# Three modulation parts of a hybrid decoder: their sums moved from VectorE to ScalarE and GpSimd

## The chip, the cores and the metric

One core of a Trainium2 chip runs the whole program. The metric is the device time of one execution in microseconds (us). PE is TensorE (matmuls), DVE is VectorE, ACT is ScalarE, POOL is GpSimd, SP is the queue that issues the DMAs here. Times given as positions are microseconds from the start of the profiled span.

## The reference

The model has two layers. Each has an attention (stick-breaking in the first layer, softmax with forgetting in the second) and a gated MLP with a short causal convolution, for 512 positions of width 1024 and 16 heads of 64. The change concerns the conditioning: a vector c of 1024 values is turned by a matrix of 1024 x 6144 for each layer into six vectors of 1024, which scale, shift and gate the two halves of the layer.

```python
c_act = jax.nn.silu(c)
for i in range(DEPTH):                                    # DEPTH = 2
    mod = jnp.einsum('bd,dm->bm', c_act, w_mod[i]) + b_mod[i]
    sh_a, sc_a, gt_a, sh_f, sc_f, gt_f = jnp.split(mod, N_MOD, axis=-1)
    h = modulate(rmsnorm(x, g_mix_pre[i]), sh_a, sc_a)
    ...                                                   # attention of h, 16 heads
    x = x + gt_a[:, None, :] * rmsnorm(o, g_mix_post[i])
    h = modulate(rmsnorm(x, g_ffn_pre[i]), sh_f, sc_f)
    ...                                                   # gated MLP of h
    x = x + gt_f[:, None, :] * rmsnorm(y, g_ffn_post[i])
```

The first attention computes, for each head and query t, weights that are a sigmoid of the score times the product of (1 - sigmoid) over the keys between; the sum of logarithms in the reference is a running product in the kernel.

## The kernel before

All matrices are float32. A float32 operand is split into a high part in the fp32r format and the rest (`split`, L191: ACT casts the high part, DVE or POOL subtracts), and each product is three matmuls (`mm3`, L264: L266, L267, L268).

**Modulation.** One part, such as GT_A of layer 0, is a sum over 1024 rows of w_mod, 1024 wide. `mod_part` (L130) loads it as eight tiles `wm` of 128 x 1024 (L139). On each partition the tile is multiplied by that partition's value of silu(c), a column of `csil`, and added into `acc` (L143; the first tile of a part with L141, unless the part is a row part whose `acc` starts from a POOL memset and the bias, L135 and L136). `acc` is then split into `ah` (ACT, L146) and `al` (DVE, L148), and two matmuls with a matrix of ones per half (L160, L161) add up the 128 partitions into `pm`. GT parts are kept as rows (L163, times the gain `gp`), the others as columns (the diagonal reads of L128, then L169 and L171). The generator yields after each tile, so that the caller decides how far a part goes at a time.

The `wm` tiles, `ah`, `al` and `gp` share one pool of three buffers (`t4`), `acc` has one buffer.

**Where the parts run.** Two parts (SH_A, SC_A of layer 0) are made by the opening `begin`, in another way. The three parts GT_A, SC_F and SH_F of layer 0 go through a `Background` that `attention` (L519) steps: three steps after each head from the third head on (L559). The remaining six go through a second `Background` inside layer 0's MLP (L831, L870), and the last, of layer 1, likewise.

**The first attention** (some 65 to 290 us). For each head and each of four query blocks TensorE makes the scores `ps` (L380), ACT two sigmoids (L389, L390), DVE a running product `om` (the scan, L391), and POOL (the two larger blocks) or DVE (the two smaller) the product `bt` (L392). In the next head's turn TensorE transposes these (`pa`, L414), ACT and DVE split the result (`ah`, `al`, L192, L193), and TensorE makes the head's output `po` (L429, L430). ACT and DVE bring it into place (`of`, L434, L435; per pair of heads split into `oh`, `ol`). Between these, a `Filler` gives TensorE the projections of later heads (`pqk`, `pv`), whose weights are loaded by SP (`wf`, L198), cast by ACT (`wh`) and subtracted by POOL (`wl`), through three buffers each; queries and keys are then split by ACT, DVE and POOL (`qa`, `qb`, L358, L359; `kh`, `kl`, L368 to L371).

**Order.** PE and SP run in the order of the program (`manual_schedule`). ACT, DVE and POOL are put in order by a planner with costs of its own; what `bg.step` issues within the attention is given a lower priority there (an offset of -100). Every engine executes its own queue strictly in order.

Of the kernel before, what the change touches and what calls it, by code (L numbers as in the profile page):

```python
# [11 lines left out]
AF = mybir.ActivationFunctionType  # L12
ALU = mybir.AluOpType
# [20 lines left out]
SH_A, SC_A, GT_A, SH_F, SC_F, GT_F = range(6)  # L34
# [3 lines left out]
def trunk(ctx, tc, x, c, w_mod, b_mod, g_mix_pre, g_mix_post, w_qkv, w_o, w_fg, b_fg,  # L38
          g_ffn_pre, g_ffn_post, w_gate, w_up, w_conv, b_conv, w_down, out):
    nc = tc.nc  # L40
# [6 lines left out]
    def nm(s):  # L47
        serial[0] += 1
        return f"{s}_{serial[0]}"

    def bank(s="b"):
        return pp.tile([P, 512], F32, tag="bank", name=nm(s), bufs=8)
# [7 lines left out]
    def t4(s, dt=F32):  # L60
        return sb.tile([P, D], dt, tag="t4", name=nm(s), bufs=3)
# [26 lines left out]
    csil = cst.tile([P, ND], F32, name="csil")  # L88
# [6 lines left out]
    def b_col(l, comp):  # L95
        return colA[:, 48 * l + 8 * comp : 48 * l + 8 * comp + 8]

    def g_col(l, comp):
        o = (96 if comp == SC_A else 112) + 8 * l
        return colA[:, o : o + 8]  # L100
# [25 lines left out]
    def diagonal(dst, src):  # L126

        nc.vector.tensor_tensor_reduce(junk(P), src, idn, 1.0, 0.0, op0=ALU.mult, op1=ALU.add, accum_out=dst)  # L128

    def mod_part(l, comp):  # L130
        row = comp in (GT_A, GT_F)
        acc = sb.tile([P, D], F32, tag="acc", name=nm("acc"), bufs=1)
        lo_c = comp * D
        if row:
            nc.gpsimd.memset(acc, 0.0)  # L135
            nc.sync.dma_start(acc[0:1, :], b_mod[l : l + 1, lo_c : lo_c + D])  # L136
        for d in range(ND):
            w = t4("wm")
            nc.sync.dma_start(w, w_mod[l, d * P : (d + 1) * P, lo_c : lo_c + D])  # L139
            if d == 0 and not row:  # L140
                nc.vector.tensor_scalar(acc, w, csil[:, 0:1], None, op0=ALU.mult)  # L141
            else:
                nc.vector.scalar_tensor_tensor(acc, w, csil[:, d : d + 1], acc, op0=ALU.mult, op1=ALU.add)  # L143
            yield
        ah = t4("ah", F32R)
        nc.scalar.copy(ah, acc)  # L146
        al = t4("al", F32R)
        nc.vector.tensor_tensor(al, acc, ah.bitcast(F32), op=ALU.subtract)  # L148
        if row:
            res = sb.tile([P, D], F32, tag="gt", name=nm("gt"), bufs=2)  # L150
            gp = t4("gp")
            g = (g_mix_post if comp == GT_A else g_ffn_post)[l]
            nc.sync.dma_start(gp, g.rearrange("(o n) -> o n", o=1).to_broadcast([P, D]))
        else:
            res = cst.tile([P, ND], F32, name=nm("mc"))
        yield
        for h in range(2):
            cs = slice(512 * h, 512 * h + 512)
            ps = bank("pm")
            nc.tensor.matmul(ps, ones, ah[:, cs], start=True, stop=False)  # L160
            nc.tensor.matmul(ps, ones, al[:, cs], start=False, stop=True)  # L161
            if row:
                nc.vector.tensor_tensor(res[:, cs], ps, gp[:, cs], op=ALU.mult)  # L163
            else:
                for j in range(4):
                    diagonal(res[:, 4 * h + j : 4 * h + j + 1], ps[:, j * P : (j + 1) * P])
            yield
        if not row:
            nc.vector.tensor_tensor(res, res, b_col(l, comp), op=ALU.add)  # L169
            if comp in (SC_A, SC_F):  # L170
                nc.vector.scalar_tensor_tensor(res, res, 1.0, g_col(l, comp), op0=ALU.add, op1=ALU.mult)  # L171
        made[l, comp] = res

    class Background:
        def __init__(self, parts):
            self.gens = [mod_part(*p) for p in parts]

        def step(self, n=1):
            while n and self.gens:
# [575 lines left out]

    cums_of = {}
    for l in range(DEPTH):
        bg = Background([(l, GT_A), (l, SC_F), (l, SH_F)] if l == 0 else [])
        scale = -0.125 if l % 2 else 0.125
        vt, qk = {}, {}  # L760
        if l == 0:
# [69 lines left out]
        bg = Background([(l, GT_F)] + ([(l + 1, c_) for c_ in (SC_A, SH_A, SC_F, SH_F, GT_A)] if l + 1 < DEPTH else []))  # L831
# [102 lines left out]
```

## Time and profile before

| | |
|---|---|
| median of 3 runs | 1308.4 us (1306.46 to 1308.93) |
| profiled execution | 1311.87 us, its span 1310.1 us |
| mean granted TensorE clock | 0.99 |
| busy of the span | PE 95%, DVE 63%, ACT 47%, POOL 22% |
| HBM | 165.92 MB read, 2.16 MB written |

How to read it: a busy share over the whole span is a mean over stages with different limits. A TensorE that is 95% busy has about 61 us in which it is not; the question for a change is which stage these lie in and what ended each wait. Rows give the line of the kernel, the engine, the operation, the output, the inputs and the shapes; an arrow to the left names what ended a wait.

### The profile page before, as it was taken

What the parts mean: (1) busy time and instruction counts of PE and PEld (TensorE: products, weight loads), DVE (VectorE), ACT (ScalarE), POOL (GpSimd) and SP (SyncE); (2) the same over time, 40 slices, a digit from 0 to 9 for tenths busy, and PEclk for the clock granted to TensorE, in tenths of its full rate; (3) what the DMA queues carried; (4) which work ended last, traced back from release to release, by engine and by line L of the source; (5) the groups of instructions that cost most, each with busy time, mean ns of one, the idle gap of its engine ahead of it and who ended that gap; (6) DMA issues with size and microseconds to landing.
All of it is one profiled execution on the core that took longest, in us unless ns stands there. A gap on an engine that the chain in (4) does not pass through costs nothing.

```text
span 1310.1 us, 17095 instructions
## 1 busy us (share of the span) xinstructions
PE 1249.2 (95%) x6244; PEld 1048.3 (80%) x6244; DVE 821.9 (63%) x1447; ACT 615.8 (47%) x1182; POOL 292.2 (22%) x326
## 2 busy tenths in 40 slices
PE   5888978999999999999999999999999999999997
PEld 3766857789888788888888789887898888888886
DVE  7778889756869887532344777786775444443233
ACT  5566745756434343321356556666753333332121
POOL 3676444641000000000023744554100000000000
PEclk8999989999999999999999999999999999999999
DMA  8653433222657776332411533332254333333321
GB/s 264 207 174 101 153 121 130 78 69 64 225 192 258 227 239 215 106 97 97 143 36 47 165 113 107 103 117 80 78 192 130 97 97 97 97 97 97 97 97 65
DMA packets 174856, 169.19 MB, mean 129 GB/s; under 512 B 6936, under 2 KB 151728, under 8 KB 174772
## 3 DMA queue, kind: packets, MB, share of 16 engines
q1 hardware_dynamic: 174596, 168.04, 40.8%
q8 instruction: 49, 0.80, 0.3%
q14 instruction: 35, 0.29, 0.1%
q10 hardware_dynamic: 176, 0.07, 0.0%
HBM read 165.92 MB, written 2.16 MB: 128 GB/s over the span
## 4 chain that ended last, share of the span: by engine, by line
PE 71%; DVE 13%; DMA 6%; ACT 5%; issue 3%; POOL 1%; SPq 0%; POOLq 0%; DVEq 0%; ACTq 0%
PE pgu L267 11%; PE pgu L268 11%; PE pgu L266 11%; PE pd L266 6%; PE pd L268 6%; PE pd L267 6%; DMA wm<-in_w_mod_dram 3%; PE pqk L266 2%; PE pqk L267 2%; PE pqk L268 2%; PE ps L380 2%; DVE acc L143 2%; PE pa L414 2%; PE po L266 1%; PE po L268 1%
## 5 line engine op out<-in xcount | busy, mean ns | idle before, releaser
L192 ACT CAST wh<-wf 128x1024 fp32r<-128x1024 f32 (+2 forms) x178 | 185.3, 1041 | 316.6 <-PE pgu L267 140.7
L193 DVE TENSOR_TENSOR wl<-wf,wh 128x1024 fp32r<-128x1024 f32 x122 | 149.2, 1223 | 217.7 <-ACT wh L192 215.6
L267 PE MATMUL pgu<-htl,wh 128*128 128x512 f32 (+1 forms) x736 | 276.4, 375 | 0.2
L266 PE MATMUL pgu<-hth,wh 128*128 128x512 f32 (+1 forms) x736 | 276.3, 375 | 0.0
L268 PE MATMUL pgu<-hth,wl 128*128 128x512 f32 (+1 forms) x736 | 276.2, 375 | 0.0
L193 POOL TENSOR_TENSOR wl<-wf,wh 128x1024 fp32r<-128x1024 f32 (+3 forms) x56 | 133.5, 2388 | 221.7 <-ACT wh L192 214.0
L267 PEld LDWEIGHTS pgu<-htl,wh 128*128 128x128 f32 x736 | 138.6, 188 | 25.5 <-DVE htl L328 0.6
L266 PEld LDWEIGHTS pgu<-hth,wh 128*128 128x128 f32 x736 | 138.6, 188 | 25.0
L268 PEld LDWEIGHTS pgu<-hth,wl 128*128 128x128 f32 x736 | 138.5, 188 | 25.0
L279 POOL TENSOR_TENSOR r<-v,mhalf 128x1 f32<-128x1 f32 x32 | 17.8, 555 | 450.0 <-DVE v L275 450.0
L143 DVE SCALAR_TENSOR_TENSOR acc<-wm,csil,acc 128x1024 f32<-128x1024 f32 x74 | 101.7, 1374 | 18.2 <-DMA wm<-in_w_mod_dram 17.5
L267 PE MATMUL pd<-wl,yh 128*128 128x512 f32 x288 | 112.0, 389 | 0.0
L266 PE MATMUL pd<-wh,yh 128*128 128x512 f32 x288 | 112.0, 389 | 0.0
L268 PE MATMUL pd<-wh,yl 128*128 128x512 f32 x288 | 112.0, 389 | 0.0
L266 PE MATMUL pqk<-hth,wh 128*128 128x512 f32 (+1 forms) x240 | 100.7, 420 | 0.3 <-DVE al L193 0.3
L268 PE MATMUL pqk<-hth,wl 128*128 128x512 f32 (+1 forms) x240 | 93.6, 390 | 0.1
L267 PE MATMUL pqk<-htl,wh 128*128 128x512 f32 (+1 forms) x240 | 93.5, 389 | 0.0
L846 ACT ACTIVATE cv<-cv 128x512 f32<-128x512 f32 x44 | 27.8, 633 | 102.6 <-DVE cv L845 98.2
L266 PE MATMUL pv<-wh,hth 128*128 128x256 f32 (+1 forms) x224 | 70.7, 316 | 1.1 <-ACT wh L192 0.6
L267 PE MATMUL pv<-wl,hth 128*128 128x256 f32 (+1 forms) x224 | 67.7, 302 | 1.2 <-POOL wl L193 1.2
L268 PE MATMUL pv<-wh,htl 128*128 128x256 f32 (+1 forms) x224 | 67.7, 302 | 0.1
L268 PEld LDWEIGHTS pd<-wh,yl 128*128 128x128 f32 x288 | 54.1, 188 | 11.3
(194 smaller groups left out, 2474.7 us busy)
## 6 DMA issues: line engine op xcount, KB each, us to landing
wm<-in_w_mod_dram SPq DMA_DIRECT2D x80, 512.0 KB, 4.9
wf<-in_w_ffn_gate_dram SPq DMA_DIRECT2D x44, 512.0 KB, 4.2
wf<-in_w_ffn_up_dram SPq DMA_DIRECT2D x44, 512.0 KB, 3.8
wf<-in_w_ffn_down_dram SPq DMA_DIRECT2D x44, 512.0 KB, 3.5
wf<-in_w_qkv_dram SPq DMA_DIRECT2D x41, 512.0 KB, 3.8
wm<-in_w_mod_dram SPq DMA_DIRECT2D x32, 256.0 KB, 4.6
wf<-in_w_o_dram SPq DMA_DIRECT2D x16, 512.0 KB, 3.5
cum<-cumd SPq DMA_DIRECT2D x16, 512.0 KB, 4.2
```

The costliest lines, as they stand in the source:

```text
L143: nc.vector.scalar_tensor_tensor(acc, w, csil[:, d : d + 1], acc, op0=ALU.mult, op1=ALU.add)
L192: nc.scalar.copy(hi, src)
L193: (engine or nc.vector).tensor_tensor(lo, src, hi.bitcast(F32), op=ALU.subtract)
L266: nc.tensor.matmul(ps, ah, bh, start=first, stop=False)
L267: nc.tensor.matmul(ps, ah, bl, start=False, stop=False)
L268: nc.tensor.matmul(ps, al, bh, start=False, stop=last)
L279: nc.gpsimd.tensor_tensor(r, v, mhalf, op=ALU.pow)
L380: nc.tensor.matmul(ps[:, :n], q[hd][:, qs], k[hd][i][:, :n], start=i == 0, stop=i == 1)
L414: nc.tensor.transpose(ps[:, (qb - kb) * P : (qb - kb + 1) * P], probs[qb][:, kb * P : (kb + 1) * P], idn)
L846: nc.scalar.activation(a, a, AF.Silu)
```

## The change

For the three parts beside the first attention, and for these alone, DVE's multiply-and-add of a tile is replaced by two instructions. ACT scales the tile by the column of `csil`: in place, or, for the first tile of a column part, directly into `acc`. POOL then adds the scaled tile to `acc`. The split of `acc`, the matmuls, the loads and their places in the program are as they were; the parts made in the MLP keep the DVE sums.

```diff
-    def mod_part(l, comp):
+    def mod_part(l, comp, beside):
...
             nc.sync.dma_start(w, w_mod[l, d * P : (d + 1) * P, lo_c : lo_c + D])
-            if d == 0 and not row:
+            if beside:
+                dst = acc if d == 0 and not row else w
+                nc.scalar.activation(dst, w, AF.Copy, scale=csil[:, d : d + 1])
+                if dst is w:
+                    nc.gpsimd.tensor_tensor(acc, acc, w, op=ALU.add)
+            elif d == 0 and not row:
                 nc.vector.tensor_scalar(acc, w, csil[:, 0:1], None, op0=ALU.mult)
             else:
                 nc.vector.scalar_tensor_tensor(acc, w, csil[:, d : d + 1], acc, op0=ALU.mult, op1=ALU.add)
...
     class Background:
-        def __init__(self, parts):
-            self.gens = [mod_part(*p) for p in parts]
+        def __init__(self, parts, beside=False):
+            self.gens = [mod_part(*p, beside) for p in parts]
...
-        bg = Background([(l, GT_A), (l, SC_F), (l, SH_F)] if l == 0 else [])
+        bg = Background([(l, GT_A), (l, SC_F), (l, SH_F)] if l == 0 else [], True)
```

## Prediction

> **What bounds the kernel now.** I read the page first: its busy shares and its chain that ended last.
>
> ```profile
> PE 1249.2 (95%) x6244; PEld 1048.3 (80%) x6244; DVE 821.9 (63%) x1447; ACT 615.8 (47%) x1182; POOL 292.2 (22%) x326
> PE 71%; DVE 13%; DMA 6%; ACT 5%; issue 3%; POOL 1%; SPq 0%; POOLq 0%; DVEq 0%; ACTq 0%
> ```
>
> TensorE bounds the whole, and DVE is second on the chain. So I looked for the stretch in which TensorE is idle, and asked for the busy times of two windows: 80 to 240 us, which holds every sum of the three modulation parts that run beside the first attention, and 240 to 300 us, the attention's end, which has none of them. The columns are the window, its length, then busy us (and instructions) by engine and the clock granted to TensorE.
>
> ```profile
> 80.00:240.00 160.00, 138.09 (x768) 115.78 (x767) 138.44 (x218) 96.09 (x213) 86.47 (x116) 0.96 0.41 135
> 240.00:300.00 60.00, 57.06 (x290) 47.25 (x288) 40.27 (x83) 37.34 (x83) 27.02 (x36) 1.00 0.28 84
> ```
>
> With the sums, TensorE idles 160 - 138.09 = 21.9 us and DVE is at 138.44/160 = 87%; without them TensorE idles 2.94 of 60 us (4.9%) and DVE is at 67%. Much of the idle time lies in a few large pieces. TensorE's timeline gives the four of over 2 us; the bracket is the idle time ahead of the instruction and what ended it.
>
> ```profile
> 168.44 0.47 PE L380 MATMUL ps<-kh,qb 128*128 128x128 f32 x1 [5.18 <-DVE om L391]
> 191.77 0.30 PE L414 MATMUL pa<-zid,bt 128*128 128x128 f32 x1 [2.66 <-DVE bt L392]
> 204.69 0.39 PE L430 MATMUL po<-al,v 128*128 128x256 f32 x1 [2.21 <-DVE al L193]
> 226.07 0.33 PE L380 MATMUL ps<-kh,qb 128*128 128x128 f32 x1 [2.42 <-DVE om L391]
> ```
>
> All four, 12.5 us together, end on a DVE instruction of the attention. What stood ahead of them on DVE, with the POOL instruction that ran beside the first:
>
> ```profile
> 161.54 1.64 DVE L143 SCALAR_TENSOR_TENSOR acc<-wm,csil,acc 128x1024 f32<-128x1024 f32 x1 [1.94 <-DMA wm<-in_w_mod_dram]
> 162.39 3.00 POOL L193 TENSOR_TENSOR wl<-wf,wh 128x1024 fp32r<-128x1024 f32 x1 [0.25 <-ACT wh L192]
> 163.11 2.82 DVE L193 TENSOR_TENSOR ol<-of,oh 128x512 fp32r<-128x512 f32 x1
> 165.86 1.27 DVE L143 SCALAR_TENSOR_TENSOR acc<-wm,csil,acc 128x1024 f32<-128x1024 f32 x1
> 167.16 1.22 DVE L391 TENSOR_TENSOR_SCAN om<-ps,zid 128x512 f32<-128x512 f32 x1
> 188.47 2.96 DVE L143 SCALAR_TENSOR_TENSOR acc<-wm,csil,acc 128x1024 f32<-128x1024 f32 x1 [0.57 <-DMA wm<-in_w_mod_dram]
> 201.28 2.42 DVE L143 SCALAR_TENSOR_TENSOR acc<-wm,csil,acc 128x1024 f32<-128x1024 f32 x1
> 221.13 1.28 DVE L143 SCALAR_TENSOR_TENSOR acc<-wm,csil,acc 128x1024 f32<-128x1024 f32 x1
> ```
>
> Each time a sum of L143 is directly or shortly ahead. The 5.18 us case shows the mechanism whole: DVE waits 1.94 us for a weight tile, sums, then its next instruction is held until POOL's ends at 165.39, sums again, and only at 167.16 gets to the scan that TensorE needs. After such an idle piece the clock is low for some microseconds:
>
> ```profile
> 168.00:172.00 4.00, 3.56 (x10) 2.75 (x11) 3.91 (x7) 1.23 (x5) 3.01 (x6) 0.50 0.21 73
> 190.00:194.00 4.00, 2.23 (x9) 1.94 (x10) 3.87 (x11) 1.01 (x2) 1.89 (x4) 0.85 0.38 99
> 194.00:198.00 4.00, 4.00 (x19) 3.32 (x18) 3.73 (x7) 2.05 (x5) 0.39 (x1) 0.73 0.22 61
> 226.00:230.00 4.00, 3.93 (x20) 3.71 (x21) 4.00 (x11) 1.81 (x8) 2.06 (x5) 0.61 0.01 4
> ```
>
> Busy time by the share not granted: 3.56 x 0.50 + 2.23 x 0.15 + 4.00 x 0.27 + 3.93 x 0.39 = 1.78 + 0.33 + 1.08 + 1.53 = 4.7 us.
>
> **The change part by part.** The rows that carry the prices, grouped by shape in the window 80 to 240 us (count, then busy us and mean ns of one, then idle time before; the line with three slashed figures is one of the whole trace, shortest, median and longest ns):
>
> ```profile
> L143 DVE SCALAR_TENSOR_TENSOR acc<-wm,csil,acc 128x1024 f32<-128x1024 f32 x22 | 35.1, 1594 | 5.4 <-DMA wm<-in_w_mod_dram 5.3
> L141 DVE TENSOR_SCALAR acc<-wm,csil 128x1024 f32<-128x1024 f32 x2 | 1.7, 872 | 0.0
> L193 DVE TENSOR_TENSOR ol<-of,oh 128x512 fp32r<-128x512 f32 x5 | 5.6, 1114 | 0.7 <-ACT oh L192 0.7
> L193 DVE TENSOR_TENSOR ol<-of,oh x16: 684/692/2823, 114.8 to 912.2; 128x512 fp32r<-128x512 f32 x16
> L148 DVE TENSOR_TENSOR al<-acc,ah 128x1024 fp32r<-128x1024 f32 x3 | 4.6, 1518 | 1.4 <-ACT ah L146 1.4
> L146 ACT CAST ah<-acc 128x1024 fp32r<-128x1024 f32 x3 | 3.1, 1041 | 0.2 <-DVE acc L143 0.2
> L193 POOL TENSOR_TENSOR wl<-wf,wh 128x1024 fp32r<-128x1024 f32 x15 | 39.4, 2628 | 23.6 <-ACT wh L192 23.3
> L392 POOL TENSOR_TENSOR bt<-bt,om 128x511 f32<-128x511 f32 x13 | 16.1, 1240 | 32.9 <-DVE om L391 28.6 <-PE pqk L268 4.3
> L392 POOL TENSOR_TENSOR bt<-bt,om 128x383 f32<-128x383 f32 x13 | 12.2, 938 | 12.0 <-DVE om L391 11.6 <-PE pa L414 0.3
> ```
>
> *Removed.* DVE loses 22 sums and 2 scalings: 35.1 + 1.7 = 36.8 us, and the 5.3 us in which it stood waiting for their tiles. That brings it to (138.4 - 36.8)/160 = 64%, which is the share it has from 240 us on. So I price the gain by that window: idle time falls from 21.9 us to 4.9% of 160 = 7.8 us, 14.1 us, and the 4.7 us of low clock goes with it: **18.8 us at most**. What is late next is TensorE itself.
>
> *Added on ACT.* Three parts of 8 tiles are 24 scalings of 128x1024. The trace shows no such scaling; the nearest row is the cast of the same shape, 1.04 us, so 24 x 1.04 = 25 us, taking ACT from 96 to 121 of 160 us (76%). In the best case the queue hides all. In the worst each scaling stands ahead of something TensorE waits for: 25 us. The new wait is ACT's for the tile's DMA, which DVE has now (5.3 us): the sigmoids and the casts of the attention stand behind it, and DVE's scans behind those. I take 2 us for the queueing and 3 of the 5.3 us for the DMA waits, which were harmful on DVE but meet a less loaded engine.
>
> *Added on POOL.* 8 + 7 + 7 = 22 additions. No row has an addition into acc; the nearest is the two-input subtraction of the same shape, wl, mean 2.63 us here and 2.39 us over the kernel:
>
> ```profile
> L193 POOL TENSOR_TENSOR wl<-wf,wh 128x1024 fp32r<-128x1024 f32 (+3 forms) x56 | 133.5, 2388 | 221.7 <-ACT wh L192 214.0
> L193 DVE TENSOR_TENSOR wl<-wf,wh 128x1024 fp32r<-128x1024 f32 x122 | 149.2, 1223 | 217.7 <-ACT wh L192 215.6
> ```
>
> 22 x 2.39 = 52.6 us take POOL from 86.5 to 139 us. If its 15 subtractions fall back to 2.39 us because the sums no longer hold them, 3.6 us come off: 135 of 160 (85%), and of the 141 us to which the window would shrink with the full gain, 96%. This is the doubtful engine. Two things of the attention stand in its queue. The first is bt, twice a head; how much room it has is seen in one head, where bt's second product ends at 152.77, DVE's last one is ready at 155.96 and TensorE's transposes start at 158.01:
>
> ```profile
> 151.91 0.86 POOL L392 TENSOR_TENSOR bt<-bt,om 128x383 f32<-128x383 f32 x1 [1.48 <-DVE om L391]
> 155.69 0.27 DVE L392 TENSOR_TENSOR bt<-bt,ps 128x127 f32<-128x127 f32 x1
> 158.01 0.60 PE L414 MATMUL pa<-zid,bt 128*128 128x128 f32 x4
> ```
>
> One addition (2.39 us) fits into 5.2 us of room, two do not. The second is wl, which has room by its buffers: three of them, and ACT's cast ahead of it is released by TensorE's use of an older tile, not by the load. With an addition running a third of the time (52.6/160) and on average half of one left, 26 products wait 26 x 0.33 x 1.2 = 10 us; I take a quarter of it as reaching TensorE, **2.5 us**. Bounds: nothing, or 22 x 2.39 = 52.6 us.
>
> *Held on DVE.* The two DVE forms that read two SBUF tensors and stay, ol (5) and al of the modulation (3), are now 1114 and 1518 ns in the mean; the shortest ol of the trace is 684 ns, so part of both is waiting for POOL already. With POOL busy 85% of the time they wait some 1 us each, 8 us less the 3 us that they wait now; half of it reaches TensorE: **2 us**. The Trainium skill, SBUF — State Buffer, section SBUF: two separate sides, says why: DVE with two SBUF inputs and GpSimd take a shared port pair as a lock, for the whole instruction. By that rule the removed sums were themselves the main contenders, which the trace bears out at 188.47 (2.96 us), so the rule cuts both ways here; the sum would be the same by rows alone.
>
> *SP and the buffers.* No DMA is added, and SP's order is that of the program. But a wm buffer is now released by POOL's addition instead of DVE's sum, after scaling plus addition, 3.43 us against 1.28 us. SP waits for these releases:
>
> ```profile
> SPq L139 <- DVE acc L143: 24.0, 9, 6.8
> L268 PE MATMUL pqk<-hth,wl 128*128 128x512 f32 (+1 forms) x240 | 93.6, 390 | 0.1
> ```
>
> Nine waits longer by 2.15 us are 19 us of SP time with attention weights queued behind. I take nothing, as these loads are two tiles ahead of TensorE's use (one tile is some 24 matmuls of 0.39 us, 9.4 us); if that cover were gone, it would be up to 19 us. The matmuls that close a part stand at fixed places of TensorE's order and would wait for a late chain too; I take nothing for it and count it with the POOL rival.
>
> *Sum.* -18.8 + 2 + 3 + 2.5 + 2 = -9.3 us, rounded up to -10 because a share of POOL's holding by the sums also goes. The profiled execution took 1311.9 us (span 1310.1), 3.5 us over the median of the three runs, 1308.4; I take the difference against the median: **1298 us**.
>
> **The rivals.**
> 1. *POOL takes DVE's place* (slower). The additions, at 96% load, stand ahead of bt and of the parts' last casts, so TensorE waits for POOL. Each one on the path costs 2.39 us; from eight (18.8/2.39) of the 22 on, the gain is gone, and with 13, one for each head in the window, it is 13 x 2.39 - 18.8 = +12: 1320 us; with ten, 1313 us. For it: the load. Against it: the 5.2 us of room, and 45 us of POOL idle time that waits for om and not the reverse. The Trainium skill, GPSIMD Engine Reference, section Engine selection, advises against two-input elementwise work on GpSimd, as about twice as slow as on VectorE; the rows agree (2388 against 1223 ns), and by that page alone this rival would lead.
> 2. *A trade* (no change). The waits for wm, now on ACT, and the held ol and al cost what the sums did: 1306 to 1311 us. For it: the 5.18 us piece was in part a DMA wait, which moves to ACT unchanged.
> 3. *All hidden.* POOL's and ACT's work lies wholly in idle time: -18.8 and up to -21 with rarer holding: 1288 us. For it: the window from 240 us on shows that TensorE can run at 95%.
>
> **How the numbers follow.** A measurement of this kernel tells about 0.2% (2.6 us) from no change. Forecast (1292 to 1305.5): 0.40; all hidden: 0.18; trade: 0.15; POOL: 0.27. Faster 0.58, same 0.15, slower 0.27. The range goes from the full gain, 1286, to ten additions on the path with some more, 1316; the likeliest case alone would span 1292 to 1305.
>
> **What would show it.** In the changed profile DVE should be near 65% in the attention window and the four idle pieces gone, with the clock at 0.98 or more. ACT's scaling should take 1.04 us, the addition 2.4 us, POOL over 80% busy. I am wrong if TensorE's waits end on POOL's bt or on the closing matmuls of a part, if ACT's waits for wm exceed 5 us, or if the additions are much longer than the subtraction.

## The result, and the profile after

The changed kernel is slower: 1328.95 us (median of 5 runs, 1327.11 to 1330.3) against 1308.93 us, ratio 1.0143 [1.0129, 1.0157]: 20 us slower, where 10 us faster was forecast. Its profiled execution took 1327.11 us, span 1325.3 us; the two profiled executions are only 15.2 us apart, because the one of before lies 2.9 us above its median and this one 1.8 us below. Line numbers after the edit are 5 to 7 higher (L391, the scan, is L398). Busy shares and chain of the changed kernel:

```profile
PE 1253.5 (95%) x6244; PEld 1050.9 (79%) x6244; DVE 789.9 (60%) x1423; ACT 641.5 (48%) x1206; POOL 336.9 (25%) x348
PE 67%; DVE 12%; ACT 6%; DMA 5%; POOL 5%; issue 3%; SPq 1%; POOLq 0%; DVEq 0%; ACTq 0%
```

POOL's share of the chain goes from 1% to 5%, though it is busy only 25% of the span. The window with the modulation parts now ends at 255 us, 15 us later; the two windows, with the columns as before:

```profile
80.00:255.00 175.00, 142.22 (x762) 118.27 (x761) 105.27 (x193) 119.54 (x232) 130.33 (x138) 0.91 0.38 120
255.00:315.00 60.00, 57.05 (x289) 47.29 (x289) 40.16 (x83) 37.56 (x82) 27.06 (x37) 1.00 0.29 86
```

The second window is that of before to a hundredth of a microsecond of TensorE time, so the loss of the profiled span (15.2 us) lies in the first. TensorE idles 32.8 us there instead of 21.9 (10.9 more), and its busy time is 4.1 us more for the same work, with the clock at 0.91 instead of 0.96. DVE is at 60%, as wanted, and POOL at 74%, less than feared. So none of the engines that feed TensorE is full, and still TensorE waits more. Its idle pieces of over 2 us (one more, at 172.26, is just 2.00):

```profile
94.39 0.44 PE L436 MATMUL po<-ah,v 128*128 128x384 f32 x1 [3.48 <-ACT ah L199]
120.60 0.33 PE L387 MATMUL ps<-kh,qb 128*128 128x128 f32 x1 [2.88 <-DVE om L398]
125.18 0.47 PE L421 MATMUL pa<-zid,bt 128*128 128x128 f32 x1 [3.40 <-DVE al L200]
188.80 0.33 PE L387 MATMUL ps<-kh,qa 128*128 128x128 f32 x1 [2.52 <-DVE om L398]
240.11 0.47 PE L387 MATMUL ps<-kh,qb 128*128 128x128 f32 x1 [8.10 <-DVE om L398]
```

The first ends on ACT: its cast stood behind a scaling that had waited for its weight tile.

```profile
92.83 1.15 ACT L142 ACTIVATE wm<-wm,csil 128x1024 f32<-128x1024 f32 x1 [3.69 <-DMA wm<-in_w_mod_dram]
93.88 0.63 ACT L199 CAST ah<-pa 128x384 fp32r<-128x384 f32 x2
```

The others end on DVE as before, but DVE now waits itself. Who waited for whom from 80 to 300 us (total us, times, longest):

```profile
ACT wm L142 <- DMA wm<-in_w_mod_dram: 16.2, 11, 3.7
ACT ah L151 <- POOL acc L144: 8.4, 2, 6.6
ACT ah L151 <- POOL bt L395: 3.1, 1, 3.1
DVE om L398 <- ACT ps L397: 17.4, 15, 2.9
DVE al L153 <- ACT ah L151: 12.7, 3, 6.9
```

In the kernel before, from 80 to 240 us, the same two DVE waits were short:

```profile
DVE om L391 <- ACT ps L390: 2.8, 5, 0.7
DVE al L148 <- ACT ah L146: 1.4, 2, 0.9
```

Two candidates stand out, both on ACT: the waits for weight tiles (16.2 us), and the wait of the cast `ah` for the last addition of a part (8.4 + 3.1 = 11.5 us). The idle piece at 94.39 is of the first kind, the largest of the second. The timeline ahead of it, ACT, POOL and DVE:

```profile
228.74 0.58 ACT L441 COPY of<-po 64x512 f32<-64x512 f32 x1
235.90 1.04 ACT L151 CAST ah<-acc 128x1024 fp32r<-128x1024 f32 x1 [6.58 <-POOL acc L144]
237.99 0.58 ACT L397 ACTIVATE ps<-ps 128x512 f32<-128x512 f32 x1
227.90 2.41 POOL L144 TENSOR_TENSOR acc<-acc,wm 128x1024 f32<-128x1024 f32 x1
231.09 4.77 POOL L144 TENSOR_TENSOR acc<-acc,wm 128x1024 f32<-128x1024 f32 x2
236.98 1.23 DVE L153 TENSOR_TENSOR al<-acc,ah 128x1024 fp32r<-128x1024 f32 x1 [6.93 <-ACT ah L151]
238.84 1.22 DVE L398 TENSOR_TENSOR_SCAN om<-ps,zid 128x512 f32<-128x512 f32 x1
```

ACT's scalings are done at 228.7; POOL has three additions left. ACT comes to `ah` and stands 6.58 us, with the next head's sigmoids behind it in its queue; DVE comes to `al` and stands 6.93 us, with the scan behind it. TensorE gets the scan at 240.1. At 125.18 and 188.80 an `al` of 2.3 us stands right ahead in DVE's queue too.

### The profile page after: what moved, and what is told of

It is laid out like the page before. It is cut to its first block, busy times and chain, and to the rows that moved or that the text cites. A ratio compares the mean times of both kernels' runs of the same rounds, so it can differ in the third digit from the quotient of the medians.

```text
span 1325.3 us, 17117 instructions
## 1 busy us (share of the span) xinstructions
PE 1253.5 (95%) x6244; PEld 1050.9 (79%) x6244; DVE 789.9 (60%) x1423; ACT 641.5 (48%) x1206; POOL 336.9 (25%) x348
## 4 chain that ended last, share of the span: by engine, by line
PE 67%; DVE 12%; ACT 6%; DMA 5%; POOL 5%; issue 3%; SPq 1%; POOLq 0%; DVEq 0%; ACTq 0%
PE pgu L274 11%; PE pgu L275 11%; PE pgu L273 11%; PE pd L273 6%; PE pd L274 6%; PE pd L275 6%; POOL acc L144 3%; PE pqk L273 2%; PE pqk L274 2%; PE pqk L275 2%; DMA wm<-in_w_mod_dram 2%; DMA wf<-in_w_ffn_gate_dram 2%; DMA wf<-in_w_qkv_dram 2%; PE ps L387 2%; PE pa L421 1%
## 5 line engine op out<-in xcount | busy, mean ns | idle before, releaser
L199 ACT CAST wh<-wf 128x1024 fp32r<-128x1024 f32 (+2 forms) x178 | 185.3, 1041 | 304.0 <-PE pd L275 134.8
L200 POOL TENSOR_TENSOR wl<-wf,wh 128x1024 fp32r<-128x1024 f32 (+3 forms) x56 | 130.4, 2331 | 205.4 <-ACT wh L199 201.2
L148 DVE SCALAR_TENSOR_TENSOR acc<-wm,csil,acc 128x1024 f32<-128x1024 f32 x52 | 66.6, 1281 | 14.2 <-DMA wm<-in_w_mod_dram 13.8
L200 DVE TENSOR_TENSOR al<-pa,ah 128x128 fp32r<-128x128 f32 (+3 forms) x128 | 60.5, 480 | 11.5 <-ACT ah L199 10.9
```

Source lines behind the costliest of these rows:

```text
L199: nc.scalar.copy(hi, src)
L200: (engine or nc.vector).tensor_tensor(lo, src, hi.bitcast(F32), op=ALU.subtract)
```

## The experiments

Ratios are to the kernel before, timed beside each, with a 95% interval. Theory A: ACT (and DVE) are blocked by the modulation; B: POOL's load delays the attention; C: DVE's instructions with two SBUF inputs are held while POOL's run, as the `al` of 2.3 us (1.23 alone) that began beside a POOL subtraction.

**The additions on DVE, the scalings on ACT.**

```diff
-                    nc.gpsimd.tensor_tensor(acc, acc, w, op=ALU.add)
+                    nc.vector.tensor_tensor(acc, acc, w, op=ALU.add)
```

> Theory A (ACT, first in the attention's chain, is blocked by the modulation: 16 us of waits for weight tiles that come late because POOL's additions hold the three buffers, and 11.5 us for the last addition ahead of the cast ah): without the POOL addition a tile is released about 1.2 us after its scaling, ACT's waits for tiles fall from 16 to 5-8 us and those of ah to under 2 us; DVE gets 22 additions of 1.2 us back and stands at 85% again. 1306 to 1316 us. Theory B (POOL's load itself delays the products bt and the weight splits): POOL falls back to 86 us of work in the window, and all of the loss goes: 1309 us or less. Theory C (the additions lock DVE's instructions with two SBUF inputs out): the 22 additions on DVE collide with POOL's splits as the sums did before; 1309 us, with the scalings on ACT for nothing.

1310.08 us, 1.0005 [0.9989, 1.0022]: all of the loss goes, though ACT still scales and still waited 8.9 us for tiles (16.2 in the changed kernel). The loss hangs on the additions being on POOL; all three theories allow that.

**The scalings on DVE, the additions on POOL.**

```diff
-                nc.scalar.activation(dst, w, AF.Copy, scale=csil[:, d : d + 1])
+                nc.vector.tensor_scalar(dst, w, csil[:, d : d + 1], None, op0=ALU.mult)
```

> ACT has no scaling and so never waits for a tile; DVE scales (24 x about 0.75 us = 18 us, half of what its sums took), POOL adds as in the changed kernel. Theory A: the 16 us of waits for tiles move to DVE, where they block the scans instead of the sigmoids, the ACT waits ahead of ah stay: 1315 to 1325 us. Theory B: POOL has the same load, so the time stays at 1326 to 1330 us. If only the ACT scalings themselves were dear (25 us of queueing), it would fall to 1305 us or less.

1331.42 us, 1.0157 [1.0133, 1.0180]: the whole loss without any scaling on ACT. The waits for `ah` were 14.6 us here.

**The split of acc on POOL.**

```diff
-        nc.scalar.copy(ah, acc)
+        if beside:
+            nc.gpsimd.tensor_scalar(ah, acc, 1.0, 1.0, op0=ALU.mult, op1=ALU.mult)
+        else:
+            nc.scalar.copy(ah, acc)
         al = t4("al", F32R)
-        nc.vector.tensor_tensor(al, acc, ah.bitcast(F32), op=ALU.subtract)
+        (nc.gpsimd if beside else nc.vector).tensor_tensor(al, acc, ah.bitcast(F32), op=ALU.subtract)
```

> The changed kernel with the split of acc (ah and al) on POOL, behind the last addition in the same queue, so that neither ACT nor DVE waits for the chain's end. Theory A: ACT's 11.5 us and DVE's 12.7 us of waits there go, TensorE's idle pieces of 8.1 and 3.4 us with them: 1315 to 1320 us. Theory B: POOL has 3 x (1.2 + 2.4) = 11 us more to do, so the time rises, 1330 to 1340 us. Theory C: al no longer meets POOL's lock on DVE (2.3 us each), 2 to 3 us faster.

1314.26 us, 1.0036 [1.0023, 1.0049]: three quarters of the loss gone with more work on POOL. Its window:

```profile
80.00:240.00 160.00, 137.84 (x751) 115.97 (x751) 100.13 (x186) 115.64 (x228) 136.96 (x139) 0.94 0.40 129
```

POOL is at 137 of 160 us, against 121 in the same window of the changed kernel, so load alone (B as I put it) does not set the time. The gain, 1.07%, is 14 us. The pieces at 125, 188 and 240 us also add up to 14.0, but that agreement is luck: this kernel has two pieces that the changed one has not, one of them behind a POOL instruction of `bt`.

```profile
179.57 0.90 PE L424 MATMUL pa<-zid,bt 128*128 128x128 f32 x3 [2.92 <-POOL bt L398]
213.05 0.58 PE L276 MATMUL pv<-wh,hth 128*128 128x256 f32 x1 [2.79 <-DVE om L401]
```

A control further down shows that the same edit gains 0.5% (7 us) in the kernel before, where ACT and DVE waited only 0.2 and 1.4 us; so between 7 and 14 us of the gain are the wait's.

**Five buffers for the tiles instead of three.**

```diff
-            w = t4("wm")
+            w = sb.tile([P, D], F32, tag="xn", name=nm("wm"), bufs=2) if beside and d % 2 else t4("wm")
```

> The changed kernel with every second tile of the three parts in the two buffers xn, which are idle during the attention: five buffers instead of three, and two of them free of ah, al and gp. Theory A: the loads are issued earlier, ACT's waits for tiles fall from 16 us to under 6 us, the waits ahead of ah stay: 1316 to 1322 us. Theory B and C: POOL's load and locks are the same, so the time stays within 3 us of 1329 us.

1328.99 us, 1.0140 [1.0117, 1.0163]: ACT's waits for tiles fell from 16.2 to 9.3 us and the time did not move. So the total of these waits is not the price of the change; the waits for `ah` (11.3 us) were still there. The idle pieces moved, though: those at 94 and 240 us are gone (1.86 us is left near 240), and two of nearly 4 us, in which the transposes wait for POOL's `bt`, stand at 104 and 186 us. What one piece costs therefore can't be read from its length.

**Only the cast ah on POOL, al on DVE.** The split on POOL as above, with the last line left on `nc.vector`.

> Only the cast ah on POOL, the subtraction al stays on DVE: ACT no longer waits for the chain's end, DVE still does, and al still meets POOL's lock. If ACT's wait is what costs: 1314 to 1317 us. If it is DVE's wait and its held al, with scans behind it: 1325 to 1330 us. If each holds the attention for itself alone: half of the gain, 1319 to 1324 us.

1326.89 us, 1.0125 [1.0095, 1.0156]: almost nothing gained. ACT is free of the wait, DVE is not, and its subtraction takes up to 3.4 us; the piece at 240 us stays:

```profile
L156 DVE TENSOR_TENSOR al<-acc,ah x3: 1225/3404/3404, 124.2 to 237.9; 128x1024 fp32r<-128x1024 f32 x3
240.41 0.48 PE L390 MATMUL ps<-kh,qb 128*128 128x128 f32 x1 [7.47 <-DVE om L401]
```

So DVE's wait alone is enough to keep the loss. Whether ACT's alone would be was not run.

**The split on POOL with five buffers, with half additions, and with every second tile.** Three variants of the kernel with the split on POOL. One takes the five buffers from above. One, by the first edit below, leaves half of the columns out of the additions. One, by the second edit, sends every second tile through ACT and POOL:

```diff
-                    nc.gpsimd.tensor_tensor(acc, acc, w, op=ALU.add)
+                    nc.gpsimd.tensor_tensor(acc[:, :512], acc[:, :512], w[:, :512], op=ALU.add)
...
-            if beside:
+            if beside and d % 2 == 0:
                 dst = acc if d == 0 and not row else w
```

> The split of acc on POOL and five buffers for the tiles. Theory A1 (what costs is that ACT and DVE stand and wait for the end of POOL's chain; with that gone, the rest of the loss is ACT's waits for tiles, 17.5 us in the kernel with the split on POOL): the waits for tiles fall to 9 us or less and the time from 1314 to 1306 to 1310 us. Theory A2 (the waits for tiles cost nothing, as with five buffers alone): 1312 to 1316 us.

> The split of acc on POOL, and each POOL addition leaves out the second half of its columns (512 instead of 1024): 22 x 1.1 = 24 us of POOL work less, everything else in place. If what is left of the loss is POOL's load (its additions ahead of bt): the waits of TensorE for bt (8 us) go and the time falls to 1300 us or less. If it is the waits of ACT for tiles: these fall only as far as buffers come free earlier, 1308 to 1313 us.

> The split of acc on POOL, and only every second tile goes through ACT and POOL; the others are summed by DVE as before the change. POOL has 10 or 11 additions less, DVE 12 sums of 1.3 us again. If POOL's load is what is left: under 1308 us, and as neither engine is near its limit, perhaps 1300 us. If every hand-over between engines in one chain costs a wait (the chain now goes from DVE to POOL and back for each tile): 1315 us or more.

Five buffers: 1310.3 us, 0.9998 [0.9984, 1.0012]. Half additions: 1299.99 us, 0.9915 [0.9890, 0.9939]. Every second tile: 1310.36 us, 1.0003 [0.9987, 1.0018]. Five buffers win some 5 us here, between what the two theories gave, so the waits for tiles may not be quite free. The half additions save 1.0036 - 0.9915, some 16 us for 24 us of POOL work (an addition takes 1.29 us at the median instead of 2.39), and TensorE's waits for POOL's `bt` fall from 6.1 + 2.2 = 8.3 us to 0.7 us. With every second tile on DVE a large piece like that of before is back (5.94 us at 171.8 us), and this middle way gains nothing.

**bt on DVE, with and without the split on POOL, and with five buffers.** `MULN` is the width up to which DVE makes the product `bt`; at 512 it makes all four of a head.

```diff
-MULN = 256
+MULN = 512
```

> The split of acc on POOL, and the two larger products bt of each head moved from POOL to DVE (their om then lies in the score's bank): POOL loses 26 products, 28 us, and everything on which the attention waits at short notice; DVE gets some 26 x 0.6 = 16 us and stands at 116 of 160 us. If what was left of the loss is bt behind POOL's additions: 1294 to 1300 us, as with half additions (1300 us), faster than before. If it is ACT's waits for tiles: 1310 to 1314 us, no gain.

> The changed kernel with only the products bt moved to DVE; the split of acc stays on ACT and DVE. If the two costs add up (the wait for the chain's end some 14 us, the products behind the additions some 12 us): 1313 to 1318 us. If POOL, freed of 28 us, is early enough at the chain's end: 1305 us or less. If only the wait for the chain's end costs: 1325 us or more.

> The same with five buffers for the tiles. With the additions off every short path, ACT's waits for tiles are what is left (10 to 17 us on ACT): 2 to 5 us faster than the same with three buffers. If they are hidden, within 2 us of it.

With the split on POOL 1300.44 us, 0.9918 [0.9896, 0.9940]; with the split as in the changed kernel 1302.44 us, 0.9929 [0.9907, 0.9952]. These two beat both the kernel before and the changed one. With the split left where it was, moving `bt` takes off 1.0143 - 0.9929, 28 us. I had expected the two costs to add up, 1313 to 1318 us for the second; instead, with `bt` off POOL the wait at the part's end nearly goes by itself, from 11.5 us to

```profile
ACT ah L151 <- POOL acc L144: 3.4, 1, 3.4
```

With five buffers as well it was 1305.41 us, 0.9951 [0.9933, 0.9970], slower than with three. The waits for tiles are again no guide; the fastest kernel that does the whole sum (`bt` on DVE, the split on POOL) has as many as the changed one:

```profile
80.00:240.00 160.00, 146.76 (x825) 123.83 (x824) 123.13 (x244) 123.19 (x247) 118.67 (x121) 0.98 0.43 135
ACT wm L142 <- DMA wm<-in_w_mod_dram: 16.1, 10, 4.3
```

TensorE idles 13.2 us in that window (21.9 before), and the clock is at 0.98. Theory C is not the main price either: the 22 additions are still on POOL in both, and with the split as in the changed kernel an `al` still takes up to 3.4 us.

**Controls: bt on DVE, and the split on POOL, each in the kernel before.**

> Control: the kernel before with only the two larger products bt moved from POOL to DVE. DVE has 138 of 160 us already and gets 16 us more (154, 96%). If the gain of the kernels with both moves comes from the exchange (sums to POOL, products to DVE): slower than before, 1315 to 1325 us. If the products on DVE are a gain of their own (no hand-over to POOL and back): 1300 to 1306 us, and the change to the modulation has no part in it.

> Control: the kernel before (sums on DVE), with the split of acc of the same three parts on POOL. If the split on POOL were a gain of its own, not the removal of the changed kernel's wait: 1300 us or less. If it only removes a wait that the change made: 1307 to 1311 us, since the sums end on DVE, and ACT and DVE waited 0.2 and 1.4 us for the split there.

bt alone: 1308.21 us, 0.9989 [0.9977, 1.0001]; DVE stands at 151 of 160 us and no time is won or lost. Neither of the two expectations came. Its window:

```profile
80.00:240.00 160.00, 140.93 (x794) 119.05 (x794) 151.28 (x251) 98.01 (x218) 58.49 (x94) 0.97 0.42 136
```

So the 0.6% (8 us) between this and the kernel that differs from it only by the modulation's move (0.9929) belong to that move. The split alone: 1304.17 us, 0.9947 [0.9928, 0.9966], between the two expectations. About half a per cent of gain is there that has nothing to do with the change, and its place I have not found (the profiled execution, span 1307.7 us, does not show it). With `bt` on DVE the same split on POOL wins only 0.1%.

**The weight splits wl on DVE, bt on POOL.**

```diff
-                ws.add(key, lambda src=src, inner=inner: w_tile(src, inner, nc.gpsimd))
+                ws.add(key, lambda src=src, inner=inner, l=l: w_tile(src, inner, nc.gpsimd if l else nc.vector))
```

> The changed kernel, bt and the split of acc as in it, but the low parts wl of the first attention's weights are subtracted by DVE instead of POOL: POOL loses some 15 x 2.4 = 36 us, DVE gets 15 x 1.22 = 18 us. If POOL's sheer load in the window was the cause (the chain of additions ends late because the queue is full): at most 1306 us, as with bt on DVE. If it was bt in POOL's queue, which is waited for at short notice and holds the additions up while it waits for its scan: 1318 us or more.

1318.72 us, 1.0082 [1.0064, 1.0100]. This takes more work off POOL (14 subtractions of 2.4 us in the window, 34 us) than moving `bt` does (26 us) and keeps more than half of the loss. Windows of this kernel and of the one with only `bt` on DVE, then this kernel's waits (80 to 260 us), TensorE's largest piece, and POOL's timeline:

```profile
80.00:240.00 160.00, 136.62 (x725) 114.80 (x724) 123.63 (x198) 112.57 (x218) 97.07 (x118) 0.89 0.39 126
80.00:240.00 160.00, 146.85 (x824) 123.61 (x822) 128.84 (x243) 125.22 (x252) 107.74 (x115) 0.98 0.43 139
POOL bt L399 <- DVE om L398: 55.1, 22, 8.9
ACT ah L151 <- POOL bt L395: 4.1, 1, 4.1
232.20 0.48 PE L387 MATMUL ps<-kh,qb 128*128 128x128 f32 x1 [6.26 <-DVE om L398]
184.06 1.09 POOL L399 TENSOR_TENSOR bt<-bt,om 128x511 f32<-128x511 f32 x1 [5.35 <-DVE om L398]
208.31 2.37 POOL L144 TENSOR_TENSOR acc<-acc,wm 128x1024 f32<-128x1024 f32 x1 [5.12 <-ACT wm L142]
```

POOL is busy 97 of 160 us and yet late at the part's end, while the kernel with `bt` on DVE has both POOL (108) and DVE (129 against 124) fuller and is some 16 us faster. So it was not the sheer load. Two reservations stand. The subtractions take 1.69 us in the mean on DVE where 1.22 was reckoned with, so this edit costs DVE 24 us in long instructions. And POOL's long wait for scans does not itself show a queue that is held up: from 80 to 240 us it is 49.8 us here, but 40.2 us in the kernel before, which has no additions, and 20.8 us in the changed one.

**What the runs settle.** The loss comes from the additions on POOL (with them on DVE it is gone) together with `bt` in the same queue: with `bt` off POOL the loss and more is gone, 28 us, while the same move in the kernel before is worth 1 us. The split off ACT and DVE takes off 14 us, of which 7 may be that edit's own gain; less load on POOL with both left in place takes off 8. I read this as three in-order queues tied into a ring: POOL's additions stand behind `bt`, which waits for DVE's scan; ACT's `ah` and DVE's `al` stand behind the last addition; the sigmoids and the scan stand behind `ah` and `al`. The last two links are seen in the timeline at 228 to 240 us. The first is argued and not shown: from 220 to 236 us POOL was busy 15.0 of 16 us, and its one `bt` there did not wait, so that at this end the additions were late because POOL was full just then. That the planner put `ah` and `al` where the additions were not yet done is seen too; why it expected them done was not tried.

## Why the prediction was wrong, point by point

*What bounds the window: right.* The sums on DVE did hold TensorE back, and lifting them is worth something: 8 us in the pair of kernels that differ in nothing else (0.9929 and 0.9989, both with `bt` on DVE), not the 18.8 us of the upper bound. A window with other work (240 to 300 us) gave too good a mark for what the busy one can reach: 13.2 us of idle time in the best kernel, not 7.8. Three figures of the working are off without bearing on this: DVE's share from 240 us on is 67% and not 64%, POOL's idle time that waits for `om` is 28.6 + 11.6 = 40.2 us and not 45, and half of 8 - 3 us is 2.5 and not 2.

*ACT's scalings: nearly right.* The form took 1.15 us and not 1.04; the addition's 2.39 us was exact:

```profile
L142 ACT ACTIVATE wm<-wm,csil x22: 1131/1152/1162, 83.2 to 227.6; 128x1024 f32<-128x1024 f32 x22
L144 POOL TENSOR_TENSOR acc<-acc,wm x22: 2338/2387/2672, 86.5 to 233.5; 128x1024 f32<-128x1024 f32 x22
```

The nearest row was a cast without a scale read from memory. The Trainium skill, ScalarE: Activation LUTs, section What ACT_TABLE_LOAD costs, gives about 93 ns for each such column operand; the rows show 1152 - 1041 = 111 ns. The waits for tiles were 16.2 us, three times DVE's 5.3, which the prediction named as a sign of being wrong, but they were not the main price: five buffers cut them to 9.3 us for nothing, and the fastest kernel that does the whole sum has 16.1.

*The step that failed* is the price of POOL's queue, in two terms. The first is the sentence on what closes a part: "The matmuls that close a part ... would wait for a late chain too; I take nothing for it". The chain's end does not reach TensorE's matmuls first (they waited 1.2 us); it reaches `ah` on ACT and `al` on DVE, two engines whose queues hold the attention. I named the new wait for the tile on ACT and missed that a sum moved from DVE to POOL makes the split, which had waited 0.2 and 1.4 us for it, a wait across engines on a chain of 2.39 us pieces (11.5 and 12.7 us). That term, set to nothing, is 7 to 14 us by the kernel with the split on POOL and its control. The second is the 2.5 us for additions ahead of `bt`: with the split on POOL, moving `bt` away saves 1.0036 - 0.9918, 15 us, and halving the additions 16 us. The two terms hang together, as `bt` off POOL alone takes off all 28 us.

*The POOL rival* was the right side and named "the parts' last casts", but I priced it by `bt`'s room ahead of the transposes and by POOL's load. The load was 74%, not 96%. And the 5.2 us of room was read from one head in a stretch (150 to 158 us) in which TensorE did not wait at all.

*GpSimd for two-input work.* By the advice of the Trainium skill that the prediction cites (GPSIMD Engine Reference, section Engine selection) the slowdown would have been forecast. But with `bt` on DVE the same additions, at the same 2.4 us, stay on POOL, and the kernel is 0.7% faster than before: the advice gave the right sign here, but the price of the addition alone does not decide.

*Held on DVE, and SP's waits.* `al` did take 2.3 us instead of 1.2 when a subtraction ran on POOL (up to 3.4 us in two experiments); what this costs by itself no run separates. TensorE waited 1.8 us in the whole program for low parts of weights, so nothing was nearly the right value for SP.

## What to carry to other kernels

Before a chain is moved to another engine, list what reads its end and look at what stands behind that reader in its own queue: a cast of 1 us that waits holds up everything queued behind it. Then look for instructions with a short deadline that share a queue with long work, such as `bt` beside the additions here; a busy share of 74% says nothing against such a place. A wait that is long in the list of waits may still be free: test it (more buffers) before building on it.

## What the runs showed that I had not expected

The split of three parts on POOL is worth 0.5% in the kernel before, with no visible cause. More buffers made one kernel faster (1.0036 to 0.9998) and another slower (0.9918 to 0.9951): each edit can give ACT, DVE and POOL a new order, and effects of a third to half a per cent may be that order's alone, which no run here tests.
